# Depthwise taps of a Conformer block: loaded ready-made instead of multiplied out on GpSimd

## The chip, the cores and the metric

The kernel runs on one core of one Trainium2 chip, as one program. The metric is the device time of an execution in microseconds. A core has a tensor engine (PE, with its weight loads as PEld), VectorE (DVE), ScalarE (ACT), GpSimd (POOL) and SyncE (SP), which here issues all DMA transfers. Each engine works through a queue of its own in order and waits on semaphores for the others.

## The reference

The kernel computes a trunk of two layers on 512 positions of width 1024, in float32. Layer 0 mixes tokens by a gated delta rule, layer 1 by a Conformer convolution; both then attend to a memory of 256 rows and apply an MLP of width 4096. The part that matters here:

```python
def causal_depthwise_conv(x, w):
    """x (B, S, C), w (W, C); out[t] = sum_j w[j] * x[t - (W-1) + j] (left zero padding)."""

def conformer_conv(h, w_pw1, b_pw1, w_dw, b_dw, ln_g, ln_b, w_pw2, b_pw2):
    u = h @ w_pw1 + b_pw1
    u = u[..., :D_MODEL] * jax.nn.sigmoid(u[..., D_MODEL:])
    c = causal_depthwise_conv(u, w_dw) + b_dw          # width 31, one filter per channel
    c = jax.nn.silu(layer_norm(c, ln_g, ln_b))
    return c @ w_pw2 + b_pw2

# reference, per layer
h = h + mixer(rms_norm(h, ...))                        # layer 0: delta rule, layer 1: conformer_conv
h = h + memory_cross_attention(rms_norm(h, ...), rms_norm(mem, ...), ...)
h = h + sq_relu_mlp(rms_norm(h, ...), ...)
# at the end: rms_norm(h, final_norm)
```

## The kernel before

Activations are kept transposed, in eight blocks of 128 channels x 512 positions (`slot()`, tiles of 128 x 512 from a pool of `NSLOT` = 66 buffers that rotate). Every large product is three matmuls on halves of the operands, high and low (`mm3`, the rows of lines 220, 221 and 222). A weight arrives as a `raw` tile of 128 x 1024, 512 KB, by SP (line 193; three buffers). ACT casts it to its high half `wh` (line 204) and DVE subtracts to the low half `wl` (the rows of line 72 named `wl<-raw,wh`); `wnext` asks for loads up to five units ahead and for splits up to three ahead. Line 72 is the body of the helper `tt`, line 75 that of `stt`, so that many operations share these lines and are told apart by their tiles.

The Python code gives the order of the work, and a scheduler then sets the order in each engine's queue by the times that it expects, so a change of one instruction can move others. "The built order" below is the order that came out of it.

At the start, the vectors and small tables `prm` are loaded in two parts (the second holds the columns behind `NVEC`, 679 KB), and the first RMS norm is taken: ACT squares the eight blocks of `x` (`sq`, line 295), DVE adds them up, and PE sums over channels by a matmul with ones (`ssq`, line 306).

In layer 1, `conformer` runs a list of units, `CONV_SEQ`: 16 of the first pointwise product ("p", PE tile `pw`, two for each channel block), then 16 of the key and value products of the memory ("k", tiles `K` and `V`). `CONV_AFTER` says behind which unit other things stand. A finished pair of pw units is evacuated by `pw_ev`: DVE multiplies by the norm (`sg`, `pa`), ACT takes the sigmoid, DVE forms the gated product. What follows depends on the block:

- Blocks 0 to 2 (`NDVE` = 3) are convolved by DVE: 31 taps each, the first on ACT, 30 on DVE as `ca<-x,prm,ca` (line 75), spread over the units by `taps_dve`. PE then transposes the result (`turn`, tile `cvT`, line 1008), and DVE adds it to `cy` and takes statistics (line 1013).
- Blocks 3 to 7 are convolved by PE. The gated product `glu` is regrouped into `xg` by 16 small DMAs on SP (line 981), and `conv` multiplies it by nine tap tiles, `TAPS[m]` (lines 1024 and 1027, PE tile `cv`). A tap tile holds, for four shifts at a time, a 32 x 32 diagonal of filter values in each place, so it is mostly zeros.

The tap tiles are made by `taps(m)`, nine products on POOL for each block: a stacked identity `ident4` times filter values from the columns `w_dw` of `prm`. `taps(3)` is called in the middle of the first MLP (in `mlp`, by the tuple passed at line 1229); `taps(4)` to `taps(7)` stand at the "t" entries of `CONV_AFTER`, behind pw units 3, 11, 13 and 14. "xg(6)" and "conv(6)" below mean these steps for block 6.

Of the kernel before, what the change touches and what calls it, by code (L numbers as in the profile page):

```python
# [11 lines left out]
ALU = mybir.AluOpType  # L12
AX = mybir.AxisListType

P = 128
NT = 512
NDVE = 3
# [6 lines left out]
OFF = {n: 8 * i for i, n in enumerate(_VECS)}  # L24
_o = 8 * len(_VECS)
# [1 line left out]
_o += 16  # L27
OFF["w_conv"] = _o
_o += 24 * 4
OFF["w_dw"] = _o  # L30
_o += 8 * 144
OFF["w_tap"] = _o
_o += NDVE * 31
OFF["out_norm"] = _o
# [3 lines left out]


@with_exitstack  # L40
def tile_trunk(ctx, tc, xT, memT, prm_d, adt_d, bdw_d, fin_d, w_ab, w_kq, w_v, w_z, w_dno, w_pw1, w_pw2,
               w_q, w_k, w_vv, w_o, w_up, w_dn, yT):
    nc = tc.nc
    pe, act, dve, pool = nc.tensor, nc.scalar, nc.vector, nc.gpsimd
# [3 lines left out]
    fsp = ctx.enter_context(tc.tile_pool(name="fsp", bufs=3))  # L48
    up = ctx.enter_context(tc.tile_pool(name="up", bufs=NSLOT))
    sp = ctx.enter_context(tc.tile_pool(name="sp", bufs=16))  # L50
# [8 lines left out]
    def slot(dt=F32, s="u", shape=(P, NT)):  # L59
        return up.tile(list(shape), dt, tag="u", name=nm(s))  # L60
# [7 lines left out]
    def const(shape, s, dt=F32):  # L68
        return cp.tile(list(shape), dt, tag=s, name=s)

    def tt(e, o, a, b, op):
        e.tensor_tensor(out=o, in0=a, in1=b, op=op)  # L72
# [16 lines left out]
    def over_c(t, n=4):  # L89
        return t.unsqueeze(1).to_broadcast([P, n, t.shape[1]])  # L90


    prm = const([P, NPRM], "prm")
# [20 lines left out]
    ident = const([P, P], "ident")  # L114
# [11 lines left out]
                       base=0, channel_multiplier=1)  # L126
    tri_gt_r = const([P, P], "tri_gt_r", F32R)
    act.copy(tri_gt_r, tri_gt)
    ident4 = const([P, 32], "ident4")
    eps_rms = const([P, 1], "eps_rms")  # L130
    pool.memset(eps_rms, EPS)
    eps_ln = const([P, 1], "eps_ln")
# [804 lines left out]

    def taps(m):

        w = OFF["w_dw"] + 144 * m  # L940
        TAPS[m] = []
        for i in range(9):
            t = slot(s="tap")
            tt(pool, t.rearrange("p (a c) -> p a c", c=32), over_c(ident4, 16),
               prm[:, w + 16 * i:w + 16 * i + 16].unsqueeze(2).to_broadcast([P, 16, 32]), ALU.mult)
            TAPS[m].append(t)

    def conformer(norm, hres, nxt):
# [115 lines left out]
        for i, (kind, u) in enumerate(CONV_SEQ):  # L1064
            if kind == "p":
                m, hf = divmod(u, 2)
                pw_mm(m, hf)
                if (m, hf) == (0, 0):
                    norm.stat()
                if (m, hf) == (1, 0):  # L1070
                    norm.spread()
                    pw_ev(0)
                if hf == 1 and m > 0:
                    pw_ev(m)
            else:
                kv_unit(1, u)
            taps_dve(5.4 if kind == "p" else 2.8)
            for what, m, *js in after.pop(i, ()):
                {"t": taps, "c": lambda m: conv(m, js), "l": lambda m: ln(), "o": ln_out, "d": turn}[what](m)
                taps_dve({"c": 2.0 * len(js)}.get(what, 0.0))  # L1080
# [11 lines left out]

    nc.sync.dma_start(out=prm[:, NVEC:NPRM], in_=prm_d[:, NVEC:NPRM])
    nc.sync.dma_start(out=adt, in_=adt_d.partition_broadcast(P))
    for b in range(4):
        bs = slice(32 * b, 32 * b + 32)
        pool.tensor_copy(ident4[bs, :], ident[bs, bs])
    abh, abl = const([P, P], "abh", F32R), const([P, P], "abl", F32R)
    act.copy(abh, wab)
    tt(dve, abl, wab, abh.bitcast(F32), ALU.subtract)  # L1100
# [64 lines left out]
    for gq in range(2):  # L1165
# [6 lines left out]
        for i in range(4):  # L1172
            h = 4 * gq + i
            m = MG[gq] + i * MSTEP[gq] // 2
# [34 lines left out]
    def do_w(m):  # L1209
        return wnext(("do", m // 2), m % 2), psum("do")  # L1210
# [11 lines left out]
    for m in range(2, 8):  # L1222
        w, ps = do_w(m)
# [3 lines left out]
    h = xattn(0, n1, h, n2)  # L1227
    n3 = Norm("cv_norm", deng=pool)
    h = mlp(0, n2, h, n3, lambda: (mem_gain(1, 0), mem_gain(1, 1), taps(3)))
    n4 = Norm("xa_norm1")  # L1230
    h = conformer(n3, h, n4)
# [47 lines left out]
    mlp(1, n5, h, None, None, finish, load)  # L1279


NSLOT = 66
NCV = 6
NRAW = 3
PRE = ((2, 4), (2, 6))
# [33 lines left out]
def _pack_a(np, w, order=None):  # L1319
    t = _tiles_a(np, w)  # L1320
    if order is not None:
        t = t[order]
    m = t.shape[0]
    return np.ascontiguousarray(t.reshape(m // 2, 2, 128, 1024).transpose(0, 2, 1, 3).reshape(m // 2, 128, 2048))


def _pack_b(np, w):
    c = w.shape[1]
    t = w.reshape(2, 4, 128, c // 512, 512).transpose(3, 0, 2, 1, 4)
    return np.ascontiguousarray(t.reshape(c // 512 * 2, 128, 2048))  # L1330


def _taps(np, w):

    wt = w.T.reshape(8, 4, 32, 31)
    e = np.zeros((4, 32, 8, 4, 9, 4), w.dtype)
    for s in range(4):
        for u in range(9):
            for r in range(4):
                d = r - s + 4 * u  # L1340
                if 0 <= d <= 30:
                    e[s, :, :, :, u, r] = wt[:, :, :, 30 - d].transpose(2, 0, 1)
    e = e.reshape(128, 8, 4, 9, 4)
    return np.concatenate([e[:, :, :, 0:8].reshape(128, 8, 128), e[:, :, :, 8].reshape(128, 8, 16)],
                          axis=2).reshape(128, 1152)


def _layout(np, i):
    i = {k: np.asarray(v) for k, v in i.items()}
    f = np.ascontiguousarray  # L1350

    def vec(v):
        return v.reshape(-1, 128).T

    r = {}
    r["xT"] = f(i["x"][0].T)
    r["memT"] = f(i["mem"][0].T.reshape(4, 2, 128, 256).transpose(0, 2, 1, 3).reshape(4, 128, 512))
    vecs = [i["dn_norm"][0], i["cv_norm"][0], i["xa_norm"][0], i["xa_norm"][1], i["xa_mem_norm"][0],
            i["xa_mem_norm"][1], i["mlp_norm"][0], i["mlp_norm"][1], i["cv_ln_g"][0],
            i["cv_ln_b"][0], i["cv_b_pw2"][0], i["cv_b_pw1"][0]]  # L1360
    cols = [vec(v) for v in vecs]
    cols.append(i["dn_w_conv"][0].T.reshape(24, 128, 4).transpose(1, 0, 2).reshape(128, 96))
    cols.append(_taps(np, i["cv_w_dw"][0]))
    cols.append(i["cv_w_dw"][0].T.reshape(8, 128, 31)[:NDVE].transpose(1, 0, 2).reshape(128, NDVE * 31))
    cols.append(i["dn_out_norm"][0].reshape(128, 1))
    r["prm"] = f(np.concatenate(cols, axis=1))
    r["adt"] = f(np.concatenate([i["dn_a_log"][0], i["dn_dt_bias"][0]]))
    r["bdw"] = f(i["cv_b_dw"][0])
    r["fin"] = f(i["final_norm"])
    w = i["dn_w_in"][0]  # L1370
    r["w_ab"] = f(w[:, 4096:].reshape(8, 128, 16).transpose(1, 0, 2).reshape(128, 128))
    r["w_kq"] = _pack_a(np, w[:, :2048], [8, 9, 10, 11, 0, 1, 2, 3, 12, 13, 14, 15, 4, 5, 6, 7])
    r["w_v"] = _pack_a(np, w[:, 2048:3072])
    r["w_z"] = _pack_b(np, w[:, 3072:4096])
    r["w_dno"] = _pack_a(np, i["dn_w_out"][0])
    r["w_pw1"] = _pack_a(np, i["cv_w_pw1"][0], [m for h in range(8) for m in (h, 8 + h)])
    r["w_pw2"] = _pack_a(np, i["cv_w_pw2"][0])
    r["w_q"] = np.stack([_pack_a(np, i["xa_w_q"][j]) for j in range(2)])
    r["w_k"] = np.stack([_pack_a(np, i["xa_w_kv"][j][:, :1024]) for j in range(2)])
    r["w_vv"] = np.stack([_pack_b(np, i["xa_w_kv"][j][:, 1024:]) for j in range(2)])  # L1380
    r["w_o"] = np.stack([_pack_a(np, i["xa_w_o"][j]) for j in range(2)])
    r["w_up"] = np.stack([_pack_a(np, i["mlp_w_up"][j]) for j in range(2)])
    r["w_dn"] = np.stack([np.concatenate([(_pack_b if (j, g) == (1, 3) else _pack_a)(
        np, i["mlp_w_down"][j][g * 1024:(g + 1) * 1024]) for g in range(4)]) for j in range(2)])
    return r
# [17 lines left out]
```

## Time and profile before

| | us |
|---|---|
| three runs | 1592.16, 1587.7, 1588.56 |
| their median | 1588.56 |
| the profiled execution, own time | 1589.25 |
| the profiled execution, span | 1587.5 |
| PE busy in the span | 1541.6 |
| DVE busy | 907.0 |
| ACT busy | 656.9 |
| POOL busy | 263.5 |

The mean granted clock of PE in the profiled execution was 0.988 of full speed. The profile is one execution; the times in its rows start at the span's start. A row of a timeline gives the start, the length, the engine, the line, the operation with its output and input tiles, and how many instructions it groups; in brackets stands an idle time before it and what ended it. A row of a group gives a count, the busy time and the mean of one in nanoseconds, and the idle time ahead. Rows for DMAs on SP's queue give the time from the first to the last issue of a group.

### The profile page before, as it was taken

What the parts mean: (1) busy time and instruction counts of PE and PEld (TensorE: products, weight loads), DVE (VectorE), ACT (ScalarE), POOL (GpSimd) and SP (SyncE); (2) the same over time, 40 slices, a digit from 0 to 9 for tenths busy, and PEclk for the clock granted to TensorE, in tenths of its full rate; (3) what the DMA queues carried; (4) which work ended last, traced back from release to release, by engine and by line L of the source; (5) the groups of instructions that cost most, each with busy time, mean ns of one, the idle gap of its engine ahead of it and who ended that gap; (6) DMA issues with size and microseconds to landing.
All of it is one profiled execution on the core that took longest, in us unless ns stands there. A gap on an engine that the chain in (4) does not pass through costs nothing.

```text
span 1587.5 us, 19586 instructions
## 1 busy us (share of the span) xinstructions
PE 1541.6 (97%) x7696; PEld 1298.6 (82%) x7696; DVE 907.0 (57%) x1288; ACT 656.9 (41%) x1004; POOL 263.5 (17%) x298
## 2 busy tenths in 40 slices
PE   9998997899999999999999999999999999999998
PEld 6777876798888888888888889888888888888886
DVE  6886878566455444343445599984545443443441
ACT  6656573745344443241324321173444432322332
POOL 1526333502111100000021316202012000000000
PEclk9999999899999999999999999999999999999999
DMA  5221113153222222322232422243212222223231
GB/s 180 67 73 60 54 42 105 52 175 107 93 66 67 87 100 93 104 96 93 96 104 93 137 88 91 73 164 101 85 41 93 93 98 101 94 93 105 95 106 53
DMA packets 46699, 147.57 MB, mean 93 GB/s; under 512 B 6288, under 2 KB 8976, under 8 KB 46608
## 3 DMA queue, kind: packets, MB, share of 16 engines
q1 hardware_dynamic: 46608, 146.33, 27.4%
q8 instruction: 60, 0.98, 0.2%
q14 instruction: 31, 0.25, 0.1%
HBM read 142.90 MB, written 2.10 MB: 91 GB/s over the span
## 4 chain that ended last, share of the span: by engine, by line
PE 85%; DVE 7%; ACT 3%; POOL 2%; issue 2%; DMA 0%; SPq 0%; DVEq 0%; POOLq 0%; ACTq 0%
PE up L220 7%; PE up L222 7%; PE up L221 7%; PE dn L220 6%; PE dn L222 6%; PE dn L221 6%; DVE ca L75 3%; PE q L220 2%; PE xo L221 2%; PE q L222 2%; PE q L221 2%; PE xo L222 2%; PE xo L220 2%; PE h L221 2%; PE pw L220 2%; PE pw L221 2%
## 5 line engine op out<-in xcount | busy, mean ns | idle before, releaser
L204 ACT CAST wh<-raw 128x1024 fp32r<-128x1024 f32 x248 | 260.5, 1052 | 705.8 <-PE dn L221 190.4
L72 DVE TENSOR_TENSOR wl<-raw,wh 128x1024 fp32r<-128x1024 f32 x248 | 312.1, 1260 | 129.7 <-ACT wh L204 123.9
L220 PE MATMUL up<-xh,wh 128*128 128x512 f32 x512 | 200.2, 391 | 0.0
L222 PE MATMUL up<-xh,wl 128*128 128x512 f32 x512 | 199.2, 389 | 0.0
L221 PE MATMUL up<-xl,wh 128*128 128x512 f32 x512 | 199.2, 389 | 0.0
L222 PE MATMUL dn<-uh,wl 128*128 128x512 f32 x448 | 174.3, 389 | 0.0
L220 PE MATMUL dn<-uh,wh 128*128 128x512 f32 x448 | 174.3, 389 | 0.0
L221 PE MATMUL dn<-ul,wh 128*128 128x512 f32 x448 | 174.3, 389 | 0.0
L72 DVE TENSOR_TENSOR h<-dn,h 128x512 f32<-128x512 f32 x56 | 41.8, 747 | 165.2 <-PE dn L222 165.2
L75 DVE SCALAR_TENSOR_TENSOR rl<-up,rb 128x512 f32<-128x512 f32 x64 | 44.2, 691 | 156.9 <-PE up L222 156.9
L72 POOL TENSOR_TENSOR tap<-ident,prm 128x512 f32<-128x512 f32 x45 | 61.9, 1406 | 329.6 <-PE up L222 263.8
L221 PEld LDWEIGHTS up<-xl,wh 128*128 128x128 f32 x512 | 96.1, 188 | 20.3 <-issue 0.5
L220 PEld LDWEIGHTS up<-xh,wh 128*128 128x128 f32 x512 | 96.1, 188 | 20.3 <-issue 0.5
L222 PEld LDWEIGHTS up<-xh,wl 128*128 128x128 f32 x512 | 96.1, 188 | 20.1
L222 PEld LDWEIGHTS dn<-uh,wl 128*128 128x128 f32 x448 | 84.1, 188 | 17.5
L220 PEld LDWEIGHTS dn<-uh,wh 128*128 128x128 f32 x448 | 84.1, 188 | 17.4
L221 PEld LDWEIGHTS dn<-ul,wh 128*128 128x128 f32 x448 | 84.1, 188 | 17.4
L72 POOL TENSOR_TENSOR sq<-sq,sq 128x512 f32<-128x512 f32 x30 | 49.9, 1664 | 252.7 <-ACT sq L295 167.8
L75 DVE SCALAR_TENSOR_TENSOR ca<-x,prm,ca 128x512 f32<-128x512 f32 x90 | 81.8, 910 | 2.1
L220 PE MATMUL h<-xh,wh 128*128 128x512 f32 x192 | 77.4, 403 | 2.1 <-ACT xh L288 2.1
L221 PE MATMUL h<-xl,wh 128*128 128x512 f32 x192 | 75.8, 395 | 0.6 <-DVE xl L75 0.6
L222 PE MATMUL h<-xh,wl 128*128 128x512 f32 x192 | 75.3, 392 | 0.0
(321 smaller groups left out, 3109.4 us busy)
## 6 DMA issues: line engine op xcount, KB each, us to landing
raw<-w_up SPq DMA_DIRECT2D x64, 512.0 KB, 3.4
raw<-w_dn SPq DMA_DIRECT2D x64, 512.0 KB, 3.5
raw<-w_pw SPq DMA_DIRECT2D x24, 512.0 KB, 3.5
raw<-w_kq SPq DMA_DIRECT2D x16, 512.0 KB, 3.6
raw<-w_k SPq DMA_DIRECT2D x16, 512.0 KB, 3.5
raw<-w_vv SPq DMA_DIRECT2D x16, 512.0 KB, 3.6
raw<-w_q SPq DMA_DIRECT2D x16, 512.0 KB, 3.4
raw<-w_o SPq DMA_DIRECT2D x16, 512.0 KB, 3.5
```

What stands on the lines that cost most here:

```text
L72: e.tensor_tensor(out=o, in0=a, in1=b, op=op)
L75: dve.scalar_tensor_tensor(out=o, in0=a, scalar=s, in1=b, op0=op0, op1=op1)
L204: act.copy(h, raw)
L220: pe.matmul(ps, wh, xh, start=first, stop=False)
L221: pe.matmul(ps, wh, xl, start=False, stop=False)
L222: pe.matmul(ps, wl, xh, start=False, stop=last)
```

## The change

The nine tap tiles of each of the blocks 3 to 7 are laid out on the host, zeros included, as a new input `tap` of 5 x 9 x 128 x 512 floats (11.8 MB). `taps(m)` no longer computes: it issues nine loads of 256 KB on SP. The `w_dw` columns of `prm` (1152 of them) and `ident4` with its four copies on POOL go away, and the pool of slots has 68 buffers in place of 66.

```diff
-OFF["w_dw"] = _o
-_o += 8 * 144
...
-    ident4 = const([P, 32], "ident4")
...
     def taps(m):
 
-        w = OFF["w_dw"] + 144 * m
         TAPS[m] = []
         for i in range(9):
             t = slot(s="tap")
-            tt(pool, t.rearrange("p (a c) -> p a c", c=32), over_c(ident4, 16),
-               prm[:, w + 16 * i:w + 16 * i + 16].unsqueeze(2).to_broadcast([P, 16, 32]), ALU.mult)
+            nc.sync.dma_start(out=t, in_=tap_d[m - NDVE, i])
             TAPS[m].append(t)
...
-    for b in range(4):
-        bs = slice(32 * b, 32 * b + 32)
-        pool.tensor_copy(ident4[bs, :], ident[bs, bs])
...
-NSLOT = 66
+NSLOT = 68
...
-    return np.concatenate([e[:, :, :, 0:8].reshape(128, 8, 128), e[:, :, :, 8].reshape(128, 8, 16)],
-                          axis=2).reshape(128, 1152)
+    e = np.concatenate([e[:, :, :, 0:8].reshape(128, 8, 128), e[:, :, :, 8].reshape(128, 8, 16)], axis=2)
+    e = e.reshape(4, 32, 8, 9, 16)[:, :, NDVE:]
+    t = np.zeros((8 - NDVE, 9, 4, 32, 16, 32), w.dtype)
+    for c in range(32):
+        t[:, :, :, c, :, c] = e[:, c].transpose(1, 2, 0, 3)
+    return t.reshape(8 - NDVE, 9, 128, 512)
...
-    cols.append(_taps(np, i["cv_w_dw"][0]))
...
+    r["tap"] = f(_taps(np, i["cv_w_dw"][0]))
```

More of the change, by code (lines that the diff above doesn't have):

```diff
@@ L40, in tile_trunk @@
 @with_exitstack
-def tile_trunk(ctx, tc, xT, memT, prm_d, adt_d, bdw_d, fin_d, w_ab, w_kq, w_v, w_z, w_dno, w_pw1, w_pw2,
+def tile_trunk(ctx, tc, xT, memT, prm_d, adt_d, bdw_d, tap_d, fin_d, w_ab, w_kq, w_v, w_z, w_dno, w_pw1, w_pw2,
                w_q, w_k, w_vv, w_o, w_up, w_dn, yT):
```

## The prediction, made before the changed kernel ran

> **What bounds the kernel now.** I read the page first, then the waits of PE around the conformer, then DVE's groups there, then single rows. The page's span, its busy line and its chain:
>
> ```profile
> span 1587.5 us, 19586 instructions
> PE 1541.6 (97%) x7696; PEld 1298.6 (82%) x7696; DVE 907.0 (57%) x1288; ACT 656.9 (41%) x1004; POOL 263.5 (17%) x298
> PE 85%; DVE 7%; ACT 3%; POOL 2%; issue 2%; DMA 0%; SPq 0%; DVEq 0%; POOLq 0%; ACTq 0%
> L72 POOL TENSOR_TENSOR tap<-ident,prm 128x512 f32<-128x512 f32 x45 | 61.9, 1406 | 329.6 <-PE up L222 263.8
> ```
>
> PE is the bound nearly everywhere, and POOL, whose 45 tap products the change takes away, is idle for 83% of the span. So 61.9 us of work vanish that nobody seems to wait for. What can come of it must be at one of PE's few stops. The views of PE's waits and rows around the conformer (900 to 1040 us) show one:
>
> ```profile
> PE K L222 <- DVE wl L72: 3.6, 1, 3.6
> 1013.00 1.21 DVE L72 TENSOR_TENSOR wl<-raw,wh 128x1024 fp32r<-128x1024 f32 x1
> 1014.26 0.58 PE L222 MATMUL K<-mh,wl 128*128 128x256 f32 x1 [3.65 <-DVE wl L72]
> ```
>
> PE stands 3.65 us for the low half of a K weight, because DVE comes to that subtract only at 1013.00. The windows (columns: length, then busy time of PE, PEld, DVE, ACT, POOL, then granted clock, DMA share, GB/s) show why it is late and what follows:
>
> ```profile
> 1000.00:1010.00 10.00, 10.00 (x91) 10.00 (x90) 9.72 (x19) 0.00 (x0) 0.64 (x1) 1.00 0.00 0
> 1013.40:1020.24 6.84, 5.98 (x28) 5.98 (x29) 6.66 (x10) 0.03 (x1) 0.00 (x0) 0.50 0.10 26
> ```
>
> DVE is full before the stop, and PE runs at half clock for 6.84 us behind it, which costs about half of them: 3.4 us. So in this one stage DVE is the bound that ends last, and the stop is worth 3.65 + 3.4 = 7.05 us.
>
> **What the products cost DVE.** DVE's groups by form, first for 910 to 941 us, where no tap product runs, then for 941 to 1001, where 36 of the 45 run:
>
> ```profile
> L75 DVE SCALAR_TENSOR_TENSOR ca<-x,prm,ca 128x512 f32<-128x512 f32 x27 | 20.2, 748 | 0.5
> L72 DVE TENSOR_TENSOR wl<-raw,wh 128x1024 fp32r<-128x1024 f32 x6 | 7.3, 1218 | 0.1
> ```
>
> ```profile
> L75 DVE SCALAR_TENSOR_TENSOR ca<-x,prm,ca 128x512 f32<-128x512 f32 x40 | 44.4, 1113 | 1.1
> L72 DVE TENSOR_TENSOR wl<-raw,wh 128x1024 fp32r<-128x1024 f32 x6 | 9.0, 1500 | 0.0
> ```
>
> The same instructions take 365 and 282 ns longer beside the products. Without them DVE has 40 x 0.365 + 6 x 0.282 = 14.6 + 1.7 = 16.3 us less to do ahead of the stop. That is the change's gain, and it is a matter of when DVE arrives, not of POOL's own time. How late DVE is now:
>
> ```profile
> 995.32 0.40 PE L222 MATMUL pw<-xh,wl 128*128 128x512 f32 x1
> 1009.62 0.68 DVE L72 TENSOR_TENSOR sg<-pw,rb 128x512 f32<-128x512 f32 x1
> ```
>
> The last pw1 unit leaves PE at 995.7, and DVE reads it at 1009.62: 13.9 us late, less than the 16.3 it is given. So I take the stop and its half clock as gone: **-7.05 us**. From below: if the slowing came from something other than the products, 0.
>
> The Trainium skill ("SBUF — State Buffer", Who interferes with whom) has a rule for this: an instruction of DVE with two inputs in SBUF contends with one of GpSimd that reads SBUF, for a shared port under an exclusive lock. By it the 36 products could hold DVE for up to their own length, an estimate of 36 x 1.406 = 50.6 us; the rows show 16.3, and the sum goes by these. The same section says that DMA never contends with an engine, by which the loads cannot give the time back to DVE; no row of before has these loads beside it.
>
> **The start.** The table's second load falls by the 1152 columns: 576 of 679 KB. Rows of the start, by engine, the window's rate and the load:
>
> ```profile
> 13.31 4.27 ACT L295 ACTIVATE sq<-x 128x512 f32<-128x512 f32 x8
> 17.52 1.06 ACT L204 CAST wh<-raw 128x1024 fp32r<-128x1024 f32 x1
> ```
>
> ```profile
> 14.54 4.67 DVE L72 TENSOR_TENSOR sq<-sq,sq 128x512 f32<-128x512 f32 x6
> 19.12 1.22 DVE L72 TENSOR_TENSOR wl<-raw,wh 128x1024 fp32r<-128x1024 f32 x1
> 20.26 0.68 DVE L72 TENSOR_TENSOR sq<-sq,sq 128x512 f32<-128x512 f32 x1
> ```
>
> ```profile
> 22.51 0.95 PE L306 MATMUL ssq<-ones,sq 128*128 128x1 f32 x8
> 9.90:13.30 3.40, 3.25 (x8) 2.03 (x9) 3.40 (x7) 3.40 (x6) 0.00 (x0) 0.50 1.03 365
> prm<-prm SPq DMA_DIRECT2D x1, 679.0 KB, 6.3
> ```
>
> 576 KB at 365 GB/s are 1.6 us: the second half of the first weights, whose cast began at 17.52, lands at about 16.0 instead. But the schedule is built on what it expects, and in the built order of the changed kernel this cast stands ahead of ACT's eight squares, not behind them; on DVE its subtract stands ahead of the six adds of squares, and the third weight's ahead of the last add. ACT is free at 13.31, so it waits for the load: cast 16.0 to 17.05, eight squares at 0.534 to 21.3. DVE: subtract to 18.3, six adds to 23.0, a subtract to 24.2, the last add to 24.9, and the sum of squares on PE, which had no wait at 22.51, begins 2.1 to 2.4 us later; I take **+2.1 us**, the smaller, since adds may overlap the squares. If the load lands at 14.2 it is +0.4, at 17.0 it is +3.2. All that follows hangs on this norm, so it is carried to the end.
>
> Does a stop of 2.1 us halve the clock too? Three windows of before:
>
> ```profile
> 83.40:86.90 3.50, 0.33 (x3) 0.00 (x1) 3.22 (x7) 3.46 (x8) 0.63 (x2) 1.00 0.26 80
> 88.40:91.80 3.40, 3.40 (x10) 2.63 (x9) 2.39 (x5) 3.31 (x7) 1.43 (x4) 0.50 0.00 0
> 219.70:221.60 1.90, 0.06 (x1) 0.00 (x0) 1.55 (x5) 1.89 (x2) 0.25 (x2) 1.00 0.00 0
> ```
>
> An idle stretch of 3.2 us was followed by 3.4 us at 0.50, one of 1.84 lay at full clock. 2.1 is nearest to the second: 0; the other end is half of 3.4, +1.7. The Trainium skill ("TensorE: Matmul & The Clock Gate", What's actually happening) puts the gate at one idle window of about 3.4 us; by it 2.1 us never halves, and the 3.2 us above should hardly have, but did.
>
> **What is late next in the conformer.** In the built order of the changed kernel DVE's third channel (30 `ca` at block 2) begins only behind the evacuation of conv(5), as its first tap on ACT now stands behind a K cast, and its transposes on PE stand one K unit later than before. Nothing is free there either. PE's rows for the pieces, and a small evacuation on DVE:
>
> ```profile
> 990.01 0.48 PE L220 MATMUL pw<-xh,wh 128*128 128x512 f32 x1
> 995.55 0.60 PE L1008 MATMUL cvT<-ident,ca 128*128 128x128 f32 x4
> 995.91 0.36 PE L220 MATMUL K<-mh,wh 128*128 128x256 f32 x1
> 998.86 1.95 PE L1024 MATMUL cv<-tap,xg 128*128 128x128 f32 x16
> 1006.82 0.36 PE L220 MATMUL K<-mh,wh 128*128 128x256 f32 x1
> L72 DVE TENSOR_TENSOR cy<-cv,cy 128x128 f32<-128x128 f32 x8 | 1.9, 276 | 0.0
> ```
>
> From start to start, the last pw unit takes 5.54 us, a channel's transposes 0.36, a K unit 2.95 and conv(6) 7.96. From the end of conv(5) to the third channel's transposes the built order has on PE that pw unit, two other channels' transposes, six K units, conv(6), and conv(7), which I take as long as conv(6): 5.54 + 2 x 0.36 + 6 x 2.95 + 2 x 7.96 = 39.9 us. DVE has in that stretch 30 x 0.748 + 6 x 1.218 + 3 x 0.7 (bias and gate of block 7, by the 0.68 of `sg`) and 12 to 16 pairs of a 276 ns evacuation and a statistic that I take as equally long: 22.4 + 7.3 + 2.1 + 6.6 to 8.8 = 38.4 to 40.6 us. So the two arrive together, and a small wait in place of the old one is likely. Its last link, a cast (1.06), a subtract (1.22) and a `ca` (0.75) behind the last but one K unit, is 3.0 us against 2.95 of PE: I take **+0.6 us**, the end of DVE's list less PE's (40.6 - 39.9) rounded down; the bounds are 0 and 3.0, where the whole link stands open.
>
> **The loads.** 45 loads of 256 KB on SP. Nearest rows, of the same size and shape:
>
> ```profile
> cy<-bdw SPq DMA_DIRECT2D x8, 256.0 KB, 6.1
> 879.77 4.32 SPq L955 DMA_DIRECT2D cy<-bdw  x8
> 962.13 10.06 SPq L981 DMA_DIRECT2D xg<-glu  x16
> 972.30 13.71 SPq L193 DMA_DIRECT2D raw<-w_k  x3
> 986.36 10.02 SPq L981 DMA_DIRECT2D xg<-glu  x16
> ```
>
> An issue takes 4.32 / 8 = 0.54 us, nine 4.9, and they land 6.1 after. taps(3) and taps(4) stand among w_dn and w_pw loads, tens of us ahead of their convolution, and a weight load that is 4.9 us late still has slots loaded ahead of it: 0 (if that cover fails, up to 4.9 each). taps(5) goes behind xg(5) and ahead of w_k loads issued from 972.30 on, whose units run from 995.91: 0. Tight is taps(6): eight of its loads stand behind xg(6) on SP, and SP has no other way. The gate of block 6, for which xg(6) waits, follows its pw unit, which leaves PE at 972.7 (the first row below), and DVE is relieved by then of some 32 of the 40 `ca`, 11.7 us at most:
>
> ```profile
> 972.30 0.40 PE L222 MATMUL pw<-xh,wl 128*128 128x512 f32 x1
> 985.58 0.74 DVE L75 SCALAR_TENSOR_TENSOR glu<-pa,prm,sg 128x512 f32<-128x512 f32 x1
> ```
>
> The gate ends now at 986.3; less 11.7 that is 974.6, and with the two passes and the subtract that stand before it on DVE I take 977. So xg(6) goes from 986.36 to 977, its 16 issues end at 987, eight loads at 991.3, and they land by 997.4; conv(6) starts at 998.86. Hidden: 0, with 1.5 us to spare.
>
> **Sum.** Span 1587.5, own time of the profiled execution 1589.25. 1589.25 - 7.05 + 0.6 + 2.1 = 1584.9. It was 0.69 above the median of the runs, 1588.56; so **1584.2 us**, 0.27% less. A measurement of this kernel can tell about 0.3% (4.8 us) from no change, so this forecast lies on the edge of being seen.
>
> **The rivals.** *The gain is taken by the new wait.* The transposes of the third channel wait the whole link, 3.0 us, and the clock halves again: -7.05 + 3.0 + 3.4 + 2.1 = +1.5, **1590.0**. For it: DVE's list against PE's has no reserve. Against: 16.3 us of relief against 13.9. With the halved clock at the start alone it is 1585.9. Chance 0.25.
> *No delay at the start.* The weights land by 14.2 us: 1584.2 - 1.7 = **1582.5**; with nothing lost there and no residual wait it is 1581.5. For it: less traffic ahead. Chance 0.12.
> *Slower: SP's order.* If DVE isn't relieved, xg(6) stays at 986.36 to 996.4, eight tap loads are issued till 1000.7 and land at 1006.8; conv(6) stops for 7.9 us, the clock halves (3.4), the old stop stays, the start is lost: 1588.56 + 7.9 + 3.4 + 2.1 = **1602**. It decides once xg(6) starts after 998.86 - 6.1 - 4.3 - 10.0 = 978.4. For it: one queue for all, and only 1.5 us to spare; a mild form, a stop of 3 us with its half clock and the start, gives 1597. Against: the rows of `ca`. Chance 0.18.
>
> **How the numbers follow.** The forecast has 0.45, with a range of its own of 1582.5 (start +0.4) to 1586.5 (residual wait or start at their upper ends). The range, 1581 to 1593, goes down to the second rival's 1581.5 and up to the first with the start at its upper ends (1590.0 + 1.1 + 1.7 = 1592.8), and leaves out the last. Faster by over 0.3% is below 1583.8: the case without delay (0.12) and half of the forecast (0.22): 0.34. Slower, above 1593.3, is the last case (0.18) and a corner of the first rival (0.02): 0.20. Within 0.3%: 0.46.
>
> **What would show it.** `ca` near 748 ns throughout 941 to 1001; no stop of K at the low half; a stop of 2 us ahead of the first sum of squares; a short one ahead of the third channel's transposes; conv(6) and conv(7) with no wait for a tap. A `ca` still at 1.1 us, a clock at half behind the start, or a DMA named as releaser of a convolution would make it wrong.

## The result, and the profile after

| | before | after |
|---|---|---|
| median of 8 runs each, us | 1589.93 (1587.04 to 1592.16) | 1583.67 (1582.41 to 1587.13) |
| ratio, 95% interval | | 0.9965 (0.9953 to 0.9977) |
| profiled execution, own time, us | 1589.25 | 1585.45 |
| span, mean granted clock | 1587.5, 0.988 | 1583.7, 0.985 |

The changed kernel is 0.35% faster. Single runs of one kernel differ by 5 us, and the clock goes with them: the runs of the changed kernel at a mean clock of 0.990 took 1582.4 to 1583.1 us, those at 0.988 took 1584.2 and 1585.6, those at 0.985 and 0.986 took 1585.5 and 1587.1. The profiled execution of after is one of the latter, so its span may not be set against that of before as a whole; the comparison has to go stage by stage.

The page of after: the span, the busy line, the chain.

```profile
span 1583.7 us, 19548 instructions
PE 1544.0 (97%) x7696; PEld 1300.6 (82%) x7696; DVE 886.9 (56%) x1288; ACT 656.2 (41%) x1004; POOL 200.2 (13%) x249
...
PE 89%; ACT 4%; DVE 3%; POOL 2%; issue 2%; DMA 1%; SPq 0%; ACTq 0%; POOLq 0%; DVEq 0%
```

POOL lost 63 us that were not on the chain. DVE lost 20 us although its 1288 instructions are the same, and its share of the chain fell from 7% to 3%: that is where the change acts. DVE's groups of after for 941 to 1001 us:

```profile
L73 DVE SCALAR_TENSOR_TENSOR ca<-x,prm,ca 128x512 f32<-128x512 f32 x41 | 30.6, 749 | 1.0
L70 DVE TENSOR_TENSOR wl<-raw,wh 128x1024 fp32r<-128x1024 f32 x6 | 7.3, 1219 | 4.8 <-PE cv L1019 4.8
```

`ca` takes 749 ns where it took 1113, `wl` 1219 where it took 1500, and DVE now even waits for PE. The waits of PE from 880 to 1062 us, and the row of the one that is left:

```profile
PE cvT L1003 <- DVE ca L73: 0.6, 1, 0.6
```

```profile
1032.72 0.66 PE L1003 MATMUL cvT<-ident,ca 128*128 128x128 f32 x4 [0.56 <-DVE ca L73]
```

The stop of 3.65 us at the K weight is gone, and a wait of 0.56 us for the third channel has come, at the place and of the size that were forecast. The windows of after show PE without a gap and at full clock where it stood and then ran at half:

```profile
1000.00:1010.00 10.00, 10.00 (x91) 10.00 (x90) 8.47 (x17) 1.77 (x2) 0.00 (x0) 1.00 0.75 278
1010.00:1020.00 10.00, 10.00 (x89) 10.00 (x88) 9.96 (x26) 2.58 (x3) 0.00 (x0) 1.00 0.36 120
```

To see where time comes and goes, I took the same matmul of PE in both traces and the difference of its starts (after less before; negative is earlier). Rows of the table are kernels, columns the place in the trace of before, the last the gain of the conformer alone:

| us | at 25 | at 320 | at 960 | at 1060 | 960 to 1060 |
|---|---|---|---|---|---|
| after | -0.40 | +2.31 | +2.26 | -3.90 | -6.16 |
| e1, before with 13 products | +0.50 | +1.69 | +1.69 | -5.49 | -7.18 |
| e2, after with 13 loads | +0.50 | +2.10 | +1.99 | -5.17 | -7.16 |
| e3, after with 66 slots | +0.34 | +1.87 | +1.80 | -4.70 | -6.50 |
| e4, after with the full table | -2.04 | -2.01 | -2.07 | -8.56 | -6.49 |
| e5, dead products | -0.40 | +2.20 | +2.11 | +4.24 | +2.13 |
| e6, dead fills | +0.49 | +1.97 | +1.89 | +3.59 | +1.70 |
| e7, rate 1.0 | -0.47 | +0.98 | +0.88 | -6.29 | -7.17 |
| e8, full table, rate 1.0 | -0.46 | -0.46 | -0.56 | -7.73 | -7.17 |
| e9, dead fills, rate 1.0 | -0.57 | +3.74 | +3.65 | -1.62 | -5.27 |
| e10, dead products, rate 1.0 | -0.25 | -0.32 | -0.41 | +4.08 | +4.49 |

The last column is the change; what comes between 25 and 320 is not. Between 25 and 320 us lies the delta rule, which the change does not touch, and there the traces differ by -0.1 to +4.3 us. The clock is what differs. Two windows of that stage, first of before, then of after:

```profile
215.00:225.00 10.00, 8.08 (x58) 7.14 (x56) 8.38 (x18) 9.18 (x16) 4.73 (x12) 1.00 0.15 49
280.00:295.00 15.00, 12.75 (x72) 10.08 (x72) 5.17 (x4) 13.86 (x29) 12.88 (x20) 0.90 0.01 2
```

```profile
215.00:225.00 10.00, 8.16 (x44) 7.14 (x43) 7.61 (x17) 9.44 (x18) 4.47 (x12) 0.83 0.13 45
280.00:295.00 15.00, 14.36 (x64) 12.63 (x65) 3.83 (x3) 13.89 (x27) 12.69 (x23) 0.67 0.01 2
```

PE is busy as long or longer and gets fewer matmuls done (44 for 58, 64 for 72), at a clock of 0.83 for 1.00 and of 0.67 for 0.90. Over all traces the shift goes with the time that the clock stood at half between 25 and 320 us (summed from the clock records): 27.3 us in before and in the three runs that shift by -0.1 to 0.0 us (e4, e8, e10), 30.7 us in the five that shift by 1.2 to 1.6, 41.0 us in after and e5 (2.7 and 2.6), 44.4 us in e9 (4.3). The Trainium skill ("TensorE: Matmul & The Clock Gate", What's actually happening) says that the gate's window is free-running and doesn't start with the kernel. By it the same stops may halve the clock in one execution and not in the next; these windows agree, as the work between them is the same in both kernels.

### The profile page after: what moved, and what is told of

It reads as the page before. It is cut to its first block, busy times and chain, and to the rows that moved or that the text cites. A ratio compares the mean times of both kernels' runs of the same rounds, so it can differ in the third digit from the quotient of the medians.

```text
span 1583.7 us, 19548 instructions
## 1 busy us (share of the span) xinstructions
PE 1544.0 (97%) x7696; PEld 1300.6 (82%) x7696; DVE 886.9 (56%) x1288; ACT 656.2 (41%) x1004; POOL 200.2 (13%) x249
## 4 chain that ended last, share of the span: by engine, by line
PE 89%; ACT 4%; DVE 3%; POOL 2%; issue 2%; DMA 1%; SPq 0%; ACTq 0%; POOLq 0%; DVEq 0%
PE up L218 7%; PE up L217 7%; PE up L219 7%; PE dn L218 6%; PE dn L217 6%; PE dn L219 6%; PE pw L217 3%; PE pw L218 3%; PE pw L219 3%; PE cv L1019 2%; PE q L217 2%; PE xo L218 2%; PE q L218 2%; PE q L219 2%; PE xo L217 2%; PE xo L219 2%
## 5 line engine op out<-in xcount | busy, mean ns | idle before, releaser
L70 DVE TENSOR_TENSOR wl<-raw,wh 128x1024 fp32r<-128x1024 f32 x248 | 308.3, 1244 | 137.5 <-ACT wh L201 127.3
L219 PEld LDWEIGHTS dn<-uh,wl 128*128 128x128 f32 x448 | 84.1, 188 | 17.5
L73 DVE SCALAR_TENSOR_TENSOR ca<-x,prm,ca 128x512 f32<-128x512 f32 x90 | 67.1, 747 | 1.6
L217 PE MATMUL q<-xh,wh 128*128 128x512 f32 x128 | 50.9, 398 | 0.0
```

The source lines that it names most:

```text
L73: dve.scalar_tensor_tensor(out=o, in0=a, scalar=s, in1=b, op0=op0, op1=op1)
L217: pe.matmul(ps, wh, xh, start=first, stop=False)
L219: pe.matmul(ps, wl, xh, start=False, stop=last)
```

## The experiments

All were timed in five rounds or more against the kernel before on the same chip: e1 to e4 on one chip, e5 to e8 on a second, e9 and e10 on a third, where before had medians of 1589.89, 1590.58 and 1590.35 us. **e1: without the products, without the loads.**

```diff
-        for i in range(9):
+        for i in range(9 if m == 3 else 1):
             t = slot(s="tap")
...
+        TAPS[m] = (TAPS[m] * 9)[:9]
```

> The kernel before with 13 tap products in place of 45: blocks 4 to 7 make one tap tile each and use it nine times, so the filter values of these blocks are left out; the second table load, the start and the 66 slots stay. Theory (the products slow DVE): ca falls from 1113 ns to near 760 between 941 and 1001 us, the stop of K and the half clock behind it go, and the time falls by 5.5 to 7 us against before, as in the changed kernel, with no load added. Rival (the gain lies in the start, the slots or the loads' place in the queues): the stop stays and the time is within 1.5 us of before.

Measured: 1583.74 us (1580.26 to 1584.46), ratio 0.9956 (0.9942 to 0.997), and `ca` as forecast by the theory:

```profile
L75 DVE SCALAR_TENSOR_TENSOR ca<-x,prm,ca 128x512 f32<-128x512 f32 x53 | 39.7, 750 | 1.5
```

PE has no wait left between 880 and 1062 us. So the absence of the products brings the whole gain: no load, no smaller table and no larger pool of slots is needed for it. (e1 also takes 32 fewer slots in turn from the pool; e9, which takes 45 more than the changed kernel, bounds what slots can do.)

**e2: the changed kernel with few loads.** The same edit on the `dma_start` of after.

> The changed kernel with 13 tap loads in place of 45, used nine times for blocks 4 to 7, whose filter values are left out. Theory (the loads are hidden): the same as the changed kernel within 1 us, 5 to 7 us below before; only the 0.6 us wait for the third channel may move with the built order. Rival (the loads cost something on SP): 1 us or more below the changed kernel, with raw weights or xg issued earlier by up to 4.9 us for each nine.

Measured: 1584.39 us (1583.22 to 1585.94), ratio 0.9967 (0.9955 to 0.998). Taking 36 loads (9.4 MB) away brings nothing that shows; in the table the conformer gains 1.0 us more than in after, 0.56 of it the wait for the third channel, which is absent here. The loads are hidden, but for at most that; how they take part in the wait is seen below.

**e3: 66 slots; e4: the start as it was.**

```diff
-NSLOT = 68
+NSLOT = 66
```

> The changed kernel with 66 slots in place of 68; the built order is the same. Theory: slots play no part, so the changed kernel's time within 1 us, 5 to 7 us below before. Rival (the two slots let the tap loads start in time): tap loads of blocks 5 to 7 are issued later, a convolution waits for a DMA, and 2 us or more of the gain go.

```diff
+_o += 8 * 144
 OFF["w_tap"] = _o
...
+    cols.append(np.zeros((128, 1152), np.float32))
```

> The 66-slot form of the changed kernel with the 1152 columns put back into the second table load (zeros that nobody reads), so the load has 679 KB again and the built order of the start is that of before: squares ahead of the second cast. Theory from the trace (the smaller load brings the second weights earlier and the new order of the start costs 0.3 us of wait): the first sum of squares at 22.0 to 22.5 with no wait, the time within 1 us of the 66-slot form. Theory of the prediction (the new order costs 2 us): 2 us below the 66-slot form.

Measured: e3 1583.89 us (1581.97 to 1584.58), ratio 0.9961 (0.9949 to 0.9974); e4 1582.71 (1580.71 to 1585.52), ratio 0.9957 (0.9944 to 0.9969). The slots play no part. The 1.2 us between e3 and e4 lie inside the scatter of either, so the runs alone don't tell what the start's order costs. Its mechanism is seen in the rows. ACT, DVE and PE at the start of after, then PE's row of e3:

```profile
13.34 1.05 ACT L201 CAST wh<-raw 128x1024 fp32r<-128x1024 f32 x1 [0.88 <-DMA raw<-w_kq]
14.30 4.27 ACT L292 ACTIVATE sq<-x 128x512 f32<-128x512 f32 x8
```

```profile
21.29 0.68 DVE L70 TENSOR_TENSOR sq<-sq,sq 128x512 f32<-128x512 f32 x1
```

```profile
22.02 1.05 PE L303 MATMUL ssq<-ones,sq 128*128 128x1 f32 x8 [0.29 <-DVE sq L70]
```

```profile
22.76 1.05 PE L303 MATMUL ssq<-ones,sq 128*128 128x1 f32 x8 [1.32 <-DVE sq L70]
```

The order is the one that was forecast, cast ahead of the squares, and ACT does wait for the load. But the load lands at 13.3 us (14.1 in e3), not at 16.0, so the sum of squares is ready at 22 us and PE waits 0.29 us for it (1.32 in e3).

What such a wait costs depends on how early PE comes to it, and so on its clock. In e4 (old order) and e7 (new order, below) the clock was 1.00 from 4.4 to 25 us, where before, after and e3 have 0.92. PE's rows, of e4, then of e7:

```profile
20.44 0.99 PE L304 MATMUL ssq<-ones,sq 128*128 128x1 f32 x8
```

```profile
21.95 1.05 PE L303 MATMUL ssq<-ones,sq 128*128 128x1 f32 x8 [1.66 <-DVE sq L70]
```

With the full clock the new order cost 1.5 us in this pair, nearly what was forecast. With 3.4 us of half clock at the start PE itself is later: the table has 0.0 and -0.5 at 25 us for the old order (before, e8), -0.6 to +0.3 for the new one. So the -2.04 of e4 is its clock and its order together, and in these traces the order costs 0 to 1.5 us, by the state of the clock.

**e5 and e6: the products back, as dead work, and fills in their place.** Each loaded tap gets a companion on POOL that nobody reads.

```diff
             nc.sync.dma_start(out=t, in_=tap_d[m - NDVE, i])
             TAPS[m].append(t)
+            f = slot(s="dead")
+            tt(pool, f.rearrange("p (a c) -> p a c", c=32), over_c(ident[:, 0:32], 16),
+               prm[:, 16 * i:16 * i + 16].unsqueeze(2).to_broadcast([P, 16, 32]), ALU.mult)   # e5
+            for _ in range(3):
+                pool.memset(f, 0.0)                                                            # e6
```

> The changed kernel with the 45 products back on POOL as dead work: same form (a broadcast identity times broadcast columns, both read from SBUF), each into a slot of its own that nobody reads. Theory (the products slow DVE): ca rises from 749 to 1000 ns or more where they run, DVE comes late again, a stop with half clock in the K units or ahead of the third channel's transposes comes back, and 4 to 8 us of the gain go, so 0 to 2 us below before. Rival (the gain comes from the loads or the queues' order): as the changed kernel, 5 to 7 us below before.

> The same with three fills (memset, which read nothing) in place of each dead product; a fill of this size took 527 ns before, so POOL is busy for 1.58 us in place of 1.41. Theory (it is POOL's reading that DVE waits for): ca stays near 750 ns and the time is that of the changed kernel within 1.5 us. Rival (any work of POOL on these slots slows DVE, or the extra slots in the rotation do): as the kernel with dead products, 4 us or more above the changed kernel.

Measured: e5 1591.95 us (1589.57 to 1595.84), ratio 1.0009 (0.9998 to 1.002); e6 1592.26 (1590.46 to 1594.14), ratio 1.0011 (1.0002 to 1.002). The gain is gone in both, for different reasons. DVE's groups of e5 and of e6, 941 to 1001 us:

```profile
L73 DVE SCALAR_TENSOR_TENSOR ca<-x,prm,ca 128x512 f32<-128x512 f32 x40 | 40.7, 1019 | 1.0
```

```profile
L73 DVE SCALAR_TENSOR_TENSOR ca<-x,prm,ca 128x512 f32<-128x512 f32 x38 | 28.4, 750 | 0.9
```

With products `ca` is slow again; with fills it is not, though POOL is as busy (33.4 us with products and 36.6 with fills of these 60). The orders of DVE's and ACT's instructions in e5 are those of after, one by one, so here the built order is no rival: the products, with the 45 slots that they take, turn the conformer's -6.16 into +2.13, by 8.3 us, slightly more than the 4 to 8 that I expected. PE's waits from 880 to 1062 us, of e5, then of e6:

```profile
PE cv L1025 <- DMA tap<-tap: 4.8, 1, 4.8
PE cvT L1006 <- DVE ca L73: 1.1, 1, 1.1
```

```profile
PE cvT L1006 <- DVE ca L73: 5.5, 1, 5.5
PE cv L1022 <- DMA xg<-glu: 0.7, 2, 0.4
```

In e5 the stop is that of the prediction's slower rival: the gate of block 6 is late, xg(6) goes out late, and conv(6) waits for tap loads that stand behind it. SP's rows, first of e5, then of after:

```profile
987.51 10.24 SPq L979 DMA_DIRECT2D xg<-glu  x16
997.86 10.88 SPq L940 DMA_DIRECT2D tap<-tap  x17
```

```profile
978.47 11.74 SPq L976 DMA_DIRECT2D xg<-glu  x16
990.32 9.64 SPq L940 DMA_DIRECT2D tap<-tap  x17
```

So the loads are hidden only because DVE is relieved. In e6 my expectation missed: DVE is as fast as in after, yet the time is lost, at the wait for the third channel. There that channel stands later in DVE's built order than in after: behind its first tap comes the evacuation of another channel, ahead of which after has six taps, and DVE idles for it:

```profile
998.08 0.29 DVE L70 TENSOR_TENSOR cy<-cvT,cy 128x128 f32<-128x128 f32 x1 [3.62 <-PE cvT L1006]
```

Whether the fills themselves had any part in it was open; e9 answers most of it.

**e7 to e10: the third channel queued earlier.** `TAP_RATE` is the rate at which DVE's taps are put among the units.

```diff
-TAP_RATE = 0.75
+TAP_RATE = 1.0
```

> The changed kernel with DVE's taps spread at 1.0 a microsecond in place of 0.75, so that the third channel is queued earlier. Theory: the wait of 0.6 us ahead of its transposes goes and nothing else moves; 0 to 1 us below the changed kernel. Rival: taps queued ahead of the gates delay glu and xg, a convolution waits, and 1 us or more is lost.

> The 66-slot form with the full table load (start in the old order) and the rate of 1.0: both small waits that the changed kernel has, ahead of the sum of squares and of the third channel's transposes, are taken away. Theory: the lowest time of all, 0 to 2 us below the changed kernel, 6 to 8 below before. Rival: the two waits lie inside half-clock stretches or are made up for, and it is the same as the changed kernel within 0.5 us.

Measured: e7 1583.03 us (1581.7 to 1585.62), ratio 0.9954 (0.994 to 0.9968); e8 1583.09 (1581.56 to 1584.24), ratio 0.9952 (0.9939 to 0.9966). The wait of 0.56 us is gone in both traces (no wait of PE between 880 and 1062 us), and the conformer's gain goes from 6.16 to 7.17. Over runs that is below what can be told: neither is shown to beat the changed kernel, and e8 is not the lowest time of all that I expected.

> The kernel with dead fills, at the tap rate of 1.0, which puts the first tap of the third channel on ACT ahead of the casts again. Theory (the fills cost nothing on DVE; the 5.5 us wait for the third channel in the kernel with fills came from that channel standing late in the built order): the wait goes, the time is that of the changed kernel at the same rate (1583.0) within 1.5 us. Rival (the fills or the extra slots in the rotation cost the time by themselves): 4 us or more above it, with the stop at another place.

> The same rate with the dead products, so that fills and products are compared in the same order of the third channel. Theory (products slow DVE by reading): ca at 1000 ns or more, xg(6) at 985 or later, the tap loads of block 6 behind it come late and conv(6) waits for a DMA by 3 to 6 us, with half clock: 4 to 8 us above the changed kernel at the same rate, near before. Rival (the products' kernel was slow by its order alone): within 1.5 us of 1583.0.

Measured: e9 1585.44 us (1583.48 to 1587.73), ratio 0.9968 (0.9956 to 0.9981); e10 1593.97 (1592.99 to 1596.48), ratio 1.0024 (1.0014 to 1.0035). PE's waits from 880 to 1062 us, of e9, then of e10, and DVE's group of e10:

```profile
PE cv L1022 <- DMA xg<-glu: 1.4, 1, 1.4
```

```profile
PE K L219 <- DVE wl L70: 3.5, 1, 3.5
PE cv L1025 <- DMA tap<-tap: 3.5, 1, 3.5
```

```profile
L73 DVE SCALAR_TENSOR_TENSOR ca<-x,prm,ca 128x512 f32<-128x512 f32 x46 | 48.3, 1053 | 0.5
```

With fills the 5.5 us wait is gone, so it was the order's, and the kernel is 8.5 us faster than with products at the same rate. It is still 2.4 us above e7, more than the 1.5 I allowed (1.9 of it lie in the conformer by the table): a 1.4 us wait for an xg transfer is part of it, and whether that comes from the 45 extra slots in the rotation or from POOL's queue, in which the small fills of xg stand behind the dead ones, was not tried. With products both stops are there at once, that of before (K behind DVE's subtract) and that of e5 (conv(6) behind its loads), and the kernel is slower than before. DVE and ACT have the same order in e10 as in e7, so again nothing differs but the products and their slots: 10.9 us by the medians, 11.7 in the conformer. e9, with as many slots, lies 1.9 us above e7 there, so the products themselves make up most of it. I had expected 4 to 8 us, and xg(6) at 985 or later, where it started at 982.90.

## Why the prediction was right

It forecast 1584.2 us in a range of 1581 to 1593, and the median is 1583.67: the fall is 0.35% where 0.27% was forecast. The likeliest case is the one that came. That the two medians lie 0.5 us apart is in part luck: the fall was 6.3 us where 4.4 was forecast, since the start cost nothing, and the eight runs put before at 1589.93, 1.4 us above the three from which the sum set out. By its steps:

- **The relief of DVE: right.** `ca` and `wl` fell to 749 and 1219 ns, and e1, e5 and e10 show that the products are the cause and that the stop hangs on it.
- **The stop and its half clock: right, the second term too large.** The stop was worth its 3.65 us. For the half clock I took half of the whole window of 6.84 us, but 0.86 us of that window (1013.40 to 1014.26) were the stop itself. The 28 matmuls behind it took 5.98 us; at the pace of a K unit (24 in 2.95 us) they take 3.4, so the term is 2.5, not 3.4. The starts of the same matmuls in both traces give 2.7: the shift goes from -1.57 at 1014.26 to -4.30 at 1020.18.
- **A term left out.** PE also waited for the V weight shortly after (0.3 us by the wait's view), and that went too. 3.65 + 2.7 + 0.3 - 0.56 = 6.1; the table has 6.16.
- **The new wait: right in its place; its size, 0.56 us for 0.6, partly by luck.** The window of after from the end of conv(5) to the third channel's transposes:

```profile
992.46:1032.72 40.26, 39.70 (x322) 38.50 (x320) 38.39 (x81) 8.62 (x10) 0.00 (x0) 1.00 0.59 205
```

PE's list is 39.70 us for the 39.9 forecast. But DVE was busy for 38.39, the lower end of my 38.4 to 40.6, where the term took the upper end. (It had 20 pairs of evacuation and statistic, not 12 to 16, but each took some 0.4 us from start to start, not 0.55.) For 1.53 us more it stood for a weight, which the term did not have (see the loads). In e3 and e4, where DVE's order in the conformer is the same, PE waits 0.2 us there. e6 shows how far the wait could have gone: 5.5 us, beyond the bound of 3.0 that I gave it, when the built order puts that channel later still.

- **The start: the step that failed is the landing of the second weights.** The time from issue to landing of this one load, in before, then in after:

```profile
raw<-w_kq SPq DMA_DIRECT2D x1, 512.0 KB, 8.2
```

```profile
raw<-w_kq SPq DMA_DIRECT2D x1, 512.0 KB, 4.9
```

It was issued at 9.33 us and landed at 17.5 in before, as the prediction had it; in after it was issued at 8.37 and landed at 13.3. So the load came 4.2 us earlier, not 1.6: 1.0 by an earlier issue, which the sum did not have, and 3.2 by a shorter time to landing, twice what 576 KB take at 365 GB/s. Why it is twice stays open, and one trace is a weak base for it: with the full table this time is 7.8, 7.0 and 7.5 us in e1, e4 and e8, with the small one 5.9 and 5.1 in e3 and e7. The chain behind the landing was right: 13.3 in place of 16.0 takes 2.7 us off the 24.9 forecast for the sum of squares, which gives 22.2, and PE began it at 22.02, after a wait of 0.29 us. The rival without a delay at the start was in this one point the better case.
- **The loads: right for conv(6), not quite nothing elsewhere.** xg(6) started at 978.47 for 977 forecast, and conv(6) had no wait. But a w_k load behind the 17 tap loads of blocks 6 and 7 came late. Rows of SP, ACT and DVE in after:

```profile
1000.29 1.07 SPq L190 DMA_DIRECT2D raw<-w_k  x2
```

```profile
1007.51 1.04 ACT L201 CAST wh<-raw 128x1024 fp32r<-128x1024 f32 x1 [5.90 <-DMA raw<-w_k]
```

```profile
1008.59 1.23 DVE L70 TENSOR_TENSOR wl<-raw,wh 128x1024 fp32r<-128x1024 f32 x1 [1.53 <-ACT wh L201]
```

In e3 that load was issued at 998.61, its cast began at 1005.64, and DVE stood 0.11 us for it. So an estimate of the loads' part in the wait of 0.56 us is what e3 lacks of it, 0.3 us; the prediction looked only at the w_k loads behind taps(5).

- **The slower rival: its condition held.** Its limit for the start of xg(6), 978.4, is moved by the shift at 960 in the table: 980.7 in after, where xg(6) started at 978.47 with no stop, and 980.5 in e5 and 978.0 in e10, where it started at 987.51 and 982.90 (SP's rows) and conv(6) stopped. Its price was too high for e5 (4.8 us of wait for 7.9), and the whole came to +2.1 us in the conformer, since the old stop did not come on top; in e10 it did, for +4.5.
- **The sum against the profiled execution.** 1584.9 forecast, 1585.45 measured, but by luck: the start cost 2.5 us less than forecast, and the delta rule, which was not in the sum, lay 2.7 us later by its clock (the table, from -0.40 at 25 us to +2.31 at 320).

## What to carry to other kernels

An engine that is idle most of the time can still slow its neighbour: compare one instruction's mean duration in a stretch with the neighbour at work and in one without, and ask whether the slowed engine is late for anything. What such a relief is worth is the lateness it takes off the one place where the bound engine stops, here 6 to 7 us out of 16 saved on DVE. The saved bytes of a load over a window's rate were no measure of how much earlier the next load lands: here 4.2 us for 1.6 forecast, in one pair of traces. And what a wait costs at one place can depend on the state of the clock ahead of it, so it has to be read in more than one trace.

## What the runs showed of the hardware that I had not expected

The view of the tile `ca` gives minimum, median and maximum of its 90 instructions, in before, then in after, then in e6:

```profile
L75 DVE SCALAR_TENSOR_TENSOR ca<-x,prm,ca x90: 730/752/1534, 906.8 to 1030.9; 128x512 f32<-128x512 f32 x90
```

```profile
L73 DVE SCALAR_TENSOR_TENSOR ca<-x,prm,ca x90: 731/749/754, 909.1 to 1031.9; 128x512 f32<-128x512 f32 x90
```

```profile
L73 DVE SCALAR_TENSOR_TENSOR ca<-x,prm,ca x90: 735/752/770, 908.7 to 1037.7; 128x512 f32<-128x512 f32 x90
```

The mean of 1113 ns hid two kinds. In the trace of before, the 17 `ca` that lie wholly beside products (by the start and end of each) have a median of 1421 ns, the 65 that touch none 751. The products are slowed as well: a median of 1050 ns for the ten with hardly any `ca` or `wl` beside them, of 1495 for the 24 nearly covered by them. Fills take 527 ns in both cases and leave `ca` alone. The Trainium skill ("SBUF — State Buffer", Who interferes with whom) says that DVE's second input contends with what GpSimd reads and not with what it only writes: e5 and e10 against e6 and e9 agree. It calls the shared port an exclusive lock. If one of the two stood for the other's whole instruction, a pair would take 0.79 + 1.01 = 1.80 us from start to start, by the distance of two `ca` clear of products (981.01 and 981.80) and of two products clear of `ca` (891.68 and 892.69). Where both run without a break, products start at 974.57, 976.02, 977.47 and 978.93 and `ca` at 975.18, 976.64, 978.09 and 979.55: they take turns, one for one, but a pair takes 1.45 us, so the two overlap in part.
